# Output projection of an encoder block as seven products of halves, with block sums of weights made in DRAM and rows transposed once

## The chip, the cores and the metric

The kernel runs on one core of a Trainium2 chip. The metric is the device time of one execution in microseconds (us). TensorE (PE) multiplies matrices from SBUF into PSUM; VectorE (DVE), ScalarE (ACT) and GpSimd (POOL) do the elementwise work; SyncE (SP) issues most transfers. Each engine runs its own instructions in program order and waits on semaphores for the others.

## The reference

One layer of a hybrid encoder: 1024 tokens (a grid of 16 rows by 64 columns), width 1024, all in float32. Half of the mixed width is a gated depthwise convolution, half an attention over a window of 8 rows by 16 columns; both meet in one output projection. Cut to what matters:

```python
h = rms_norm(x, norm1_g)
z = h @ w_in                                   # conv a, gate; q, k, v
u = a * sigmoid(gate)
y = layer_norm(depthwise_conv31(u) + dw_bias, conv_ln_g, conv_ln_b)
conv = silu(y)                                 # (S, 512)
attn = neighbourhood_attention(q, k, v, rpb)   # (S, 512)
x = x + concat([conv, attn]) @ w_out           # output projection, (S, 1024) @ (1024, 1024)
h2 = rms_norm(x, norm2_g)
x = x + (silu(h2 @ w_gate) * (h2 @ w_up)) @ w_down   # inner width 2816
```

## The kernel before

Every float32 operand of the large products is split into a high and a low part (`split`, L103: a cast on ACT, a subtraction on POOL or DVE). `mac` (L110) makes a block product of three matmuls, 128x128 against 128x512: high by high, high by low, low by high.

**Order in time.** The program is one list written out by hand. norm1, the input projection and the convolution's taps fill the first 227 us; the taps run on DVE, some side taps on ACT and POOL (`side_taps`, L330). The loop at L789 is the attention: 32 steps (half a grid of rows, a block of columns, a pair of heads) in a pipeline. In iteration i, scores of step i are multiplied on PE (`score_mm`), those of step i-1 are scaled on POOL (`score_norm`, L637), those of i-2 are transposed on PE (`flip`, L646) and evacuated on DVE and ACT (`flip_out`, L651), step i gets its bias on DVE and its exponential on ACT (L628, L630), and step i-3 is multiplied with the values (`weigh`, L662). Every fourth step a result is evacuated (`evac_hi`, `evac_lo`). Weights of the output projection are loaded by SP (`issue`) and split in between (`take`, `take_parts`, L156).

**Output projection.** For each of 8 token tiles `t` and each half `d` of the width, `proj` (L723) runs over 8 blocks `k` of 128 (4 of the convolution, 4 of attention): 8 x 2 x 8 x 3 = 384 matmuls into one PSUM tile (`pj`, `pk`). Between its blocks `weave` inserts prepared work: `conv_T` transposes the convolution's output into rows (L728), `conv_stats` and `conv_scale` normalise it, `conv_silu` transposes it back. `resid` (L774) adds the result to the rows `x2`, once for each tile and half. `norm2` and `norm2_out` (L856, L863) make the normed rows `xn`. `t2_one` (L994) transposes the first four tiles (32 transposes).

**Gate and up.** The 1024x1024 by 1024 products of each pair of column blocks are made as seven products of halves, m1 to m7 (`product`, L1013; `evac`, L1024): on the rows' side they use A11, A12, A22 and the sums S1 to S4 (`s_sum`, made on rows, then transposed by `s_T`, L963, 80 transposes), on the weights' side sums of weight blocks made by DVE (`t_sums`, L893) and split (`prep`). The last stage does the same for the down projection.

## Time and profile before

| | us |
|---|---|
| median of three runs | 1064.31 (1063.71 to 1064.37) |
| the profiled execution | 1064.03 |
| its span | 1062.2 |
| PE busy | 1045.4 |
| DVE, ACT, POOL busy | 699.8, 443.7, 397.3 |

The stages follow each other on PE: up to about 227 us norm, projection and taps; to 317 attention; to 421 output projection and norm2; to 850 gate and up; to the end the down projection. Busy time is the time in which at least one instruction was under way; consecutive matmuls overlap, so the distance of their starts is what each of them takes. A row of the timeline gives start and duration in us, engine, line, operation, output<-inputs, shape, count of merged instructions, and in brackets the idle time before it and what ended it. A row of the groups gives count, then busy time in us and mean ns of one, then idle time before. A row of the windows gives for each engine busy us and instructions in the stretch, then the granted clock of PE as a share of full speed, the transfers' share and their rate.

### The profile page before, as it was taken

Reading aid. Unit: us, or ns where it says so; the run is one execution under the profiler, and the core shown is the slowest. Engines: PE = TensorE matmul, PEld = TensorE weight load, DVE = VectorE, ACT = ScalarE, POOL = GpSimd, SP = SyncE. Lnnn points to the kernel's source line nnn. Section 1 sums busy time; section 2 is a strip of 40 time slices with the busy share of each in tenths; the row PEclk is TensorE's granted clock in tenths of the full one; section 3 lists DMA queues with packets and bytes.
Section 4 is the critical chain, followed back from the end, with each engine's and each line's share of the span. In section 5 each row is a group of like instructions: output and inputs, shape, how many; then the busy total and the mean of one; then the engine's idle time right before and its main releaser. Section 6 shows DMA issues by size and latency. Waiting matters only on the chain.

```text
span 1062.2 us, 13969 instructions
## 1 busy us (share of the span) xinstructions
PE 1045.4 (98%) x5068; PEld 847.3 (80%) x5068; DVE 699.8 (66%) x1072; ACT 443.7 (42%) x874; POOL 397.3 (37%) x308
## 2 busy tenths in 40 slices
PE   7999999999999999999999999999999999999997
PEld 5788888776667888788888888888888888888886
DVE  6768998966765247666565564564655567858883
ACT  6456346626776334532323223332233344433441
POOL 0126568823542301444554544545454200002310
PEclk9999999999999999999999999999999999999999
DMA  9416681245504412032322222232132597634641
GB/s 333 164 47 225 217 257 36 75 161 154 165 34 161 136 80 99 21 129 77 136 91 104 109 99 95 104 129 100 70 131 78 194 322 276 209 99 132 205 127 43
DMA packets 68244, 144.05 MB, mean 136 GB/s; under 512 B 12496, under 2 KB 21200, under 8 KB 67536
## 3 DMA queue, kind: packets, MB, share of 16 engines
q1 hardware_dynamic: 66336, 139.95, 38.3%
q10 hardware_dynamic: 1840, 3.22, 0.9%
q8 instruction: 40, 0.66, 0.3%
q14 instruction: 28, 0.23, 0.1%
HBM read 103.99 MB, written 44.76 MB: 140 GB/s over the span
## 4 chain that ended last, share of the span: by engine, by line
PE 94%; DMA 2%; DVE 1%; ACT 1%; POOL 1%; issue 0%; SPq 0%; POOLq 0%; ACTq 0%
PE B L112 6%; PE B L114 6%; PE B L113 6%; PE A L112 4%; PE D L112 4%; PE D L114 4%; PE A L114 4%; PE D L113 4%; PE A L113 4%; PE z L113 3%; PE z L112 3%; PE z L114 3%; PE gl L114 3%; PE gl L112 3%; PE gl L113 3%; PE o L662 2%
## 5 line engine op out<-in xcount | busy, mean ns | idle before, releaser
L319 DVE SCALAR_TENSOR_TENSOR cv<-u,par,cv 128x1009 f32<-128x1009 f32 (+14 forms) x85 | 108.5, 1276 | 1.9
L345 POOL TENSOR_TENSOR pa<-pa,pr 128x1022 f32<-128x1022 f32 (+10 forms) x31 | 74.2, 2392 | 35.5 <-ACT pr L344 26.5
L104 ACT CAST op<-sr 128x512 fp32r<-128x512 f32 x77 | 47.7, 619 | 52.1 <-PE B2d L114 26.3
L108 DVE TENSOR_TENSOR op<-sr,op 128x512 fp32r<-128x512 f32 x77 | 57.1, 742 | 16.1 <-ACT op L104 16.0
L1037 DVE TENSOR_TENSOR g<-B,g 128x512 f32<-128x512 f32 x22 | 15.2, 691 | 79.0 <-PE B L114 79.0
L1209 POOL TENSOR_TENSOR ou<-ou,resm 128x512 f32<-128x512 f32 x8 | 12.2, 1530 | 144.0 <-DMA resm<-xd 142.1
L1046 ACT ACTIVATE D<-D 128x512 f32<-128x512 f32 x22 | 12.8, 582 | 113.1 <-DVE D L1045 113.1
L1032 DVE TENSOR_TENSOR u<-B,g 128x512 f32<-128x512 f32 x22 | 15.2, 691 | 62.1 <-PE B L114 62.1
L104 ACT CAST op<-wd 128x512 fp32r<-128x512 f32 x66 | 40.9, 620 | 30.7 <-DVE wd L1124 18.4
L637 POOL TENSOR_SCALAR e<-e,rs 128x288 f32<-128x288 f32 (+1 forms) x64 | 34.1, 545 | 50.2 <-DVE rs L635 42.9
L108 DVE TENSOR_TENSOR op<-wd,op 128x512 fp32r<-128x512 f32 x66 | 50.4, 764 | 1.8
L893 DVE TENSOR_TENSOR ts<-gu,ts 128x512 f32<-128x512 f32 x44 | 51.0, 1159 | 0.8
L1035 ACT ACTIVATE A<-A 128x512 f32<-128x512 f32 x20 | 11.6, 582 | 76.3 <-PE A L114 76.3
L630 ACT ACTIVATE e<-e,mx 128x288 f32<-128x288 f32 (+1 forms) x64 | 36.2, 569 | 2.0 <-DVE mx L628 2.0
L628 DVE CUSTOM_DVE_ANT_0 e<-s,tab 128x288 f32<-128x288 f32 (+1 forms) x64 | 30.1, 505 | 8.1 <-PE s L615 8.0
L344 ACT ACTIVATE pr<-u,par 128x1022 f32<-128x1022 f32 (+10 forms) x31 | 34.2, 1135 | 1.2 <-ACT vs L405 1.2
L893 DVE TENSOR_TENSOR ts<-gu 128x512 f32<-128x512 f32 x22 | 34.1, 1551 | 0.0
L646 PEld LDWEIGHTS p<-ident,e 128*96 128x96 f32 (+1 forms) x192 | 20.1, 133 | 15.2 <-issue 10.5
L944 POOL TENSOR_TENSOR xn<-xn,xn 128x512 f32<-128x512 f32 x4 | 6.9, 1732 | 57.3 <-DVE sn L944 57.3
L646 PE MATMUL p<-ident,e 128*96 128x128 f32 (+1 forms) x192 | 27.6, 280 | 0.7 <-DVE pT L651 0.6
L662 PE MATMUL o<-pT,vw 96*64 96x128 f32 (+1 forms) x384 | 28.0, 281 | 0.0
L615 PE MATMUL s<-kT,qT 64*128 64x288 f32 (+1 forms) x128 | 26.7, 495 | 0.0
(1039 smaller groups left out, 3449.6 us busy)
## 6 DMA issues: line engine op xcount, KB each, us to landing
gu<-in_gu SPq DMA_DIRECT2D x44, 512.0 KB
sr<-sd SPq DMA_DIRECT2D x77, 256.0 KB
sd<-sd SPq DMA_DIRECT2D x22, 512.0 KB
wd<-in_wd SPq DMA_DIRECT2D x44, 256.0 KB
sd<-g SPq DMA_DIRECT2D x33, 256.0 KB
x<-in_x SPq DMA_DIRECT2D x16, 512.0 KB
xd<-x SPq DMA_DIRECT2D x8, 512.0 KB
resm<-xd SPq DMA_DIRECT2D x16, 256.0 KB
```

The costliest lines, as they stand in the source:

```text
L104: act.copy(hi, src)
L108: eng.tensor_tensor(*[w[..., sl] for w in (lo, src, hi.bitcast(F32))], OP.subtract)
L112: pe.matmul(acc, lh, rh, start=start, stop=False, skip_group_check=True)
L113: pe.matmul(acc, lh, rl, start=False, stop=False, skip_group_check=True)
L114: pe.matmul(acc, ll, rh, start=False, stop=stop, skip_group_check=True)
L319: dve.scalar_tensor_tensor(acc[:, o], uc[:, i], dwk[:, c, t:t + 1], acc[:, o], OP.mult, OP.add)
L344: act.activation(pr[:, o], uc[:, i], AF.Copy, scale=dwk[:, c, t:t + 1])
L345: pool.tensor_tensor(pa[:, o], pa[:, o], pr[:, o], OP.add)
L630: act.activation(e[:, hh], e[:, hh], AF.Exp, bias=mx, scale=-1.0, accum_out=rs[:, hh:hh + 1])
L646: pe.transpose(pt[:m, g * P:(g + 1) * P], es[i][:, hh, g * m:(g + 1) * m], ident)
L662: pe.matmul(os_[s_][hh * HD:(hh + 1) * HD, hp], vw[cb, rh + g][:, c:c + HD], pTs[i][:, g, hh], start=g == 0, stop=g == 2)
L893: dve.tensor_tensor(o, l, r, OP.subtract)
```

## The change

**Seven products.** The output projection becomes seven products of halves, n1 to n7. On the activations' side: `a11` (attention of the second half of the grid rows), A22 and A12 (the convolution of the two halves) and four combinations Q1 to Q4, made of `rowf` (attention of the first half) and `diff` in place and split by POOL. On the weights' side the blocks B11, B21, B22 and sums P1 to P4. Each product is 4 tiles x 4 blocks x 3 matmuls, 336 in all; a result goes into one or two of the rows' halves (`put`, 40 instructions, where `resid` had 16).

**Block sums in DRAM.** P1 to P4 of the output weights (`w4`) and of the first four gate/up blocks (`g4`) are made in DRAM by `sum_steps`: SP copies one block (12 transfers: two halves for each sum of w4, one for each of g4), POOL adds another with an accumulating transfer (12 as well). P2 starts from P1 and P4 from P2, so these wait for each other; the steps stand iterations or products apart, by the numbers in the loops. `t_sums` then serves blocks 4 to 21 only, and all of `prep`'s splits go to POOL.

**Convolution norm.** Its transposes, statistics, inverse root (three Newton steps on DVE in place of ACT's root) and scaling stand in the attention loop. `conv_silu` stays in the projection, with 12 subtractions or additions that put it into `diff` and `rowf`.

**Rows transposed once.** `turn` transposes the normed rows of all tiles (64 transposes, 16 groups of 4); the sums S1 to S4 are made from the transposed copies by DVE and POOL, and `s_split` splits them. The first four gate/up blocks take their products in another order, and signs of some sums are turned.

```diff
...
+    def sum_steps(w, parts):
+        h = P // parts
+
+        def put_(n, m, i):
+            return lambda: nc.sync.dma_start(pw[w, n][i * h:i * h + h], block(w, m)[i * h:i * h + h])
+
+        def add(n, m, i):
+            return lambda: pool.dma_start(pw[w, n][i * h:i * h + h], block(w, m)[i * h:i * h + h], accum_op=OP.add,
+                                          max_dma_last_dim=2048)
+        both = range(parts)
+        head = [put_(n, "B12", i) for n in ("P1", "P3") for i in both]
+        head += [add(n, m, i) for n, m in (("P1", "B11"), ("P3", "B22")) for i in both]
+        tail = [f(n, m, i) for n, l, r in (("P2", "P1", "B22"), ("P4", "P2", "B21"))
+                for f, m in ((put_, l), (add, r)) for i in both]
+        head.insert(7, tail.pop(0)) if parts == 2 else None
+        return head + tail
...
-            at[cb] = [G(f"at{cb}{w}", F32R).rearrange("p (c t q) -> p c t q", c=4, t=2) for w in range(2)]
-        act.copy(at[cb][0][:, :, rh], os_[s_])
-
-    def evac_lo(s_, cs=slice(0, 4)):
+            if not rowf:
+                rowf.extend(G(f"rf{j}").rearrange("p (c b q) -> p c b q", c=2, b=4) for j in range(2))
+            for j in range(2):
+                act.copy(rowf[j][:, :, cb], os_[s_][:, 2 * j:2 * j + 2])
+        else:
+            a11[cb] = [w.rearrange("p (c q) -> p c q", c=4) for w in lr(G(f"a11{cb}", F32R))]
+            act.copy(a11[cb][0], os_[s_])
...
-        hi, lo = [w[:, cs, rh] for w in at[cb]]
-        dve.tensor_tensor(lo, os_[s_][:, cs], hi.bitcast(F32), OP.subtract)
+        if rh == 0:
+            return
+        if not diff:
+            diff.extend(G(f"df{j}").rearrange("p (c b q) -> p c b q", c=2, b=4) for j in range(2))
+        for j in js:
+            cs = slice(2 * j, 2 * j + 2)
+            hi, lo = [w[:, cs] for w in a11[cb]]
+            dve.tensor_tensor(lo, os_[s_][:, cs], hi.bitcast(F32), OP.subtract)
+            dve.tensor_tensor(diff[j][:, :, cb], os_[s_][:, cs], rowf[j][:, :, cb], OP.subtract)
...
+    LHS = {"n7": "Q3", "n4": "A22", "n6": "Q2", "n5": "Q1", "n2": "A12", "n3": "Q4"}
+    RHS = {"n1": "B11", "n7": "P3", "n4": "P4", "n6": "P2", "n5": "P1", "n2": "B21", "n3": "B22"}
+    CB = (0, 3, 1, 2)
+
+    def proj(p, cb, acc, cs=range(4), start=True):
+        w = wq[RHS[p]]
+        for c in cs:
+            mac(acc, lhs(p, c, cb), [w[:, o + c * 512:o + c * 512 + 512] for o in (0, 2048)],
...
+    def q_split(n, f, j, eng):
+        if j == 0:
+            qop[n] = H(n, F32R)
+        split(*[qop[n][:, o + j * 1024:o + j * 1024 + 1024] for o in (0, 2048)],
+              f[j].rearrange("p c b q -> p (c b q)"), (eng,))
...
+    mvs = par[:, 8:24].rearrange("p (t n) -> p t n", n=2)
...
+    def conv_norm(t):
+        y = conv_T(t)
+        st6 = SM(f"bs{t}", 6)
         dve.bn_stats(st6, y)
-        dve.bn_aggr(mv, st6)
-        act.activation(sd, mv[:, 1:2], AF.Sqrt, bias=eps)
-        cs[t] = y, mv, sd
-        if 1 <= t <= 4:
-            conv_scale(t - 1)
-        if t >= 4:
-            conv_scale(t)
-
-    def conv_scale(t):
-        y, mv, sd = cs.pop(t)
-        r = SM(f"br{t}", 1)
-        dve.reciprocal(r, sd)
+        dve.bn_aggr(mvs[:, t], st6)
         if t % 2 == 0:
-            xx = G(f"xh{t}")
-            xh.extend([xx[:, :512], xx[:, 512:]])
-        if t >= 6:
-            dve.tensor_scalar(xh[t], y, mv[:, 0:1], r, op0=OP.subtract, op1=OP.mult)
-        else:
-            nb = SM(f"bb{t}", 1)
-            dve.scalar_tensor_tensor(nb, mv[:, 0:1], -1.0, r, OP.mult, OP.mult)
-            act.activation(xh[t], y, AF.Identity, bias=nb, scale=r)
+            xh.extend(lr(G(f"xh{t}")))
+        act.copy(xh[t], y)
...
+    def rsqrt(out, v, name):
+        n = v.shape[-1]
+        w, g, q = SM(name + "w", n), SM(name + "g", n), SM(name + "q", n)
+        dve.tensor_scalar(w, v, EPS, None, op0=OP.add)
+        dve.tensor_scalar(g.bitcast(I32), w.bitcast(I32), 1, None, op0=OP.logical_shift_right)
+        dve.tensor_scalar(g.bitcast(I32), g.bitcast(I32), -1.0, float(0x5F3759DF), op0=OP.mult, op1=OP.add)
+        yield
+        for i in range(3):
+            if i == 2:
+                yield
+            dve.tensor_tensor(q, g, g, OP.mult)
+            dve.scalar_tensor_tensor(q, q, 0.25 ** i, w, OP.mult, OP.mult)
+            dve.scalar_tensor_tensor(g, q, -3.0, g, OP.add, OP.mult)
+        dve.tensor_scalar(out, g, -0.125, None, op0=OP.mult)
+        yield
+
+    def conv_scale(t, eng):
+        eng.tensor_scalar(xh[t], xh[t], mvs[:, t, 0:1], rc[:, t:t + 1], op0=OP.subtract, op1=OP.mult)
...
+    def conv_diff(h, c, y4):
+        tiles = lambda w: w.rearrange("p (b i j) -> p i b j", b=4, j=16)
+        d, r = [tiles(w[c // 2][:, c % 2].rearrange("p b q -> p (b q)")) for w in (diff, rowf)]
+        dve.tensor_tensor(d, y4, d, OP.subtract if h else OP.add)
+        if h == 0:
+            dve.tensor_tensor(r, r, y4, OP.subtract)
...
-    def resid(t, d, acc):
-        dve.tensor_tensor(x2[t][:, d * 512:(d + 1) * 512], acc, x2[t][:, d * 512:(d + 1) * 512], OP.add)
-
-    acc0, xh = [], []
-
-    def attn_half(t):
-        acc0.append(mm(f"pj{t}"))
-        proj(t, 0, acc0[t], range(4, 8))
-
-    def fill(*ks):
-        if not acc0:
-            act.activation(warm, eps, AF.Sqrt)
-            acc0.append(mm("pj0"))
-        proj(0, 0, acc0[0], ks)
+    def put(t, d, acc, op=OP.add, eng=dve):
+        w = x2[t][:, d * 512:(d + 1) * 512]
+        eng.tensor_tensor(w, w, acc, op)
...
+    def read(p, cb):
+        acc = pb[cb]
+        if p == "n1":
+            put(4 + cb, 0, acc)
+            put(4 + cb, 1, acc, OP.subtract)
+        elif p == "n7":
+            put(cb, 1, acc, OP.subtract)
+            put(cb, 0, acc)
+        elif p in ("n4", "n6"):
+            put(cb, 0, acc, OP.add if p == "n4" else OP.subtract)
+        elif p == "n5":
+            put(cb, 1, acc)
+            put(4 + cb, 1, acc)
+            norm2(cb)
+        elif p == "n2":
+            put(4 + cb, 0, acc)
+        else:
+            put(4 + cb, 1, acc)
+            norm2(4 + cb)
...
-        if i in (14, 22):
-            take_parts(jobs)
+        if i in (13, 17, 21, 25):
+            take_parts(jobs, more=i < 21)
+        if i in (2, 4, 9, 11, 16, 18):
+            aside_sum()
+        if i in (3, 6, 13, 21, 28):
+            gate_sum()
+        if i in (32, 33):
+            issue()
...
+        if i % 3 == 0 and i < 27:
+            conv_norm(i // 3 - 1)
+        if i == 25:
+            root = rsqrt(rc, mvs[:, :, 1], "rc")
+        if 25 <= i < 28:
+            next(root)
+        if 28 <= i < 32:
+            conv_scale(2 * i - 56, dve)
+            conv_scale(2 * i - 55, dve)
+        if i == 33:
+            act.activation(warm, eps, AF.Silu)
+            conv_silu(0, 0)
...
-    products = [(i, p) for p in ("m1", "m2", "m6", "m5", "m7", "m4", "m3") for i in range(2)]
-    products += [(i, p) for i in range(2, FB) for p in ORDER]
+    products = [(i, p) for k in (0, 2) for p in ("m1", "m2") for i in (k, k + 1)]
+    products += [(i, p) for k in (0, 2) for p in SRC for i in (k, k + 1)]
+    products += [(i, p) for i in range(4, FB) for p in ORDER]
...
+    def turn(t, j):
+        if not h2:
+            h2.extend(H(f"h2{w}", F32R).rearrange("p (k s) -> p k s", s=512) for w in range(2))
+        pt = (tp, mm)[j](f"t2{t}{j}")
+        for i in range(4):
+            kb = 4 * j + i
+            pe.transpose(pt[:, i * P:(i + 1) * P], xn[t][:, kb * P:(kb + 1) * P], ident)
+        if j == 0:
+            xT[t] = G(f"xT{t}")
+        w = lr(xT[t])[j]
+        if t < 4:
+            hi, lo = [q[:, 4 * j:4 * j + 4, t * P:(t + 1) * P] for q in h2]
+            p3 = pt.rearrange("p (k s) -> p k s", s=P)
+            act.copy(hi, p3)
+            act.copy(w, pt)
...
+    def group(p, cbs=CB):
+        for cb in cbs:
+            more = p in ("n7", "n5")
+            if not more:
+                pb[cb] = mm(f"{p}{cb}")
+            proj(p, cb, pb[cb], start=not more)
+            read(p, cb)
...
+    weaves(12, s0=lambda: (weigh(31), evac_hi(7), evac_lo(7)), s1=QS("Q3", diff, 0, pool), s2=lambda: tails.pop()(), s3=lambda: read("n1", 0),
+           s4=QS("Q3", diff, 1, pool), s6=C(0, 1), s10=take)
+    group("n1", CB[1:])
+    for cb in CB:
+        load_x2(cb)
+    gate_sum()
+    weaves(16, s1=C(0, 2), s5=take, s9=C(0, 3), s13=QS("Q2", diff, 0, pool))
+    group("n7")
+    weaves(16, s0=C(1, 0), s2=QS("Q2", diff, 1, pool), s4=take, s6=C(1, 1), s9=take, s12=QS("Q1", rowf, 0, pool))
+    group("n4")
+    gate_sum()
+    weaves(16, s0=C(1, 2), s2=take, s5=C(1, 3), s7=QS("Q1", rowf, 1, pool), s10=take, s13=QS("Q4", diff, 0, pool))
+    group("n6")
+    weaves(16, s1=take, s3=QS("Q4", diff, 1, pool), s6=take, s9=N(0), s13=N(3))
+    group("n5")
+    gate_sum()
+    while pos[0] < len(chunks):
+        issue()
+    for _ in range(3):
+        next_raw()
+    weaves(16, s0=take, s1=[N(1), U(0, 0)], s2=U(0, 1), s3=[lo2, lo2], s4=U(3, 0), s5=[U(3, 1), N(2)], s6=[lo2, lo2],
+           s7=U(1, 0), s8=U(1, 1), s9=[lo2, lo2, prep], s10=[U(2, 0), take], s11=U(2, 1), s12=[lo2, lo2], s13=prep)
+    group("n2")
+    weaves(16, s3=prep, s7=prep, s9=N(4), s12=U(4, 0), s13=[U(4, 1), N(7)], s15=SS(0, 1, 2))
+    group("n3")
...
+        0: dict(s0=U(7, 0), s1=[U(7, 1), N(5)], s2=SP("S2", 0), s3=SS(3, 1, 2)),
+        1: dict(s0=U(5, 0), s1=[U(5, 1), N(6)], s2=SP("S2", 3), s3=SS(1, 1, 2)),
+        2: dict(s0=U(6, 0), s1=[U(6, 1), lambda: act.activation(warm, eps, AF.Silu)], s2=SP("S2", 1), s3=SS(2, 1, 2)),
+        3: dict(s0=SP("S2", 2), s2=SP("S1", 0), s3=SP("S1", 3)),
...```

Three places in the engines' orders follow: instruction, output<-inputs, shape, count. First POOL in attention, iterations 15 to 18, before: score scalings (L637) with splits of the output weights between some.

```order
L637 TENSOR_SCALAR e14_2540<-e14_2540,rs14_2541 128x288 x2
L637 TENSOR_SCALAR e15_2574<-e15_2574,rs15_2575 128x288 x2
L108 TENSOR_TENSOR wo04_2523<-wo04r_1627,wo04_2523 128x256
L637 TENSOR_SCALAR e16_2607<-e16_2607,rs16_2608 128x384 x2
L108 TENSOR_TENSOR wo04_2523<-wo04r_1627,wo04_2523 128x256
L637 TENSOR_SCALAR e17_2641<-e17_2641,rs17_2642 128x384 x2
```

and after:

```order
L677 TENSOR_SCALAR e14_2609<-e14_2609,rs14_2610 128x288 x2
L118 TENSOR_TENSOR wB11_2558<-B110r_1637,wB11_2558 128x256
L212 DMA w4P4_68<-in_w4 256x512
L677 TENSOR_SCALAR e15_2644<-e15_2644,rs15_2645 128x288 x2
L118 TENSOR_TENSOR wB11_2558<-B110r_1637,wB11_2558 128x256
L677 TENSOR_SCALAR e16_2689<-e16_2689,rs16_2690 128x384 x2
L118 TENSOR_TENSOR wB11_2558<-B111r_1748,wB11_2558 128x256
L212 DMA w4P4_68<-in_w4 256x512
L677 TENSOR_SCALAR e17_2724<-e17_2724,rs17_2725 128x384 x2
```

A split stands in each iteration, and the two accumulating transfers of P4 (L212) stand ahead of the scaling of steps 15 and 17.

Second DVE in attention around step 28, before (bias with running maximum L628, flip evacuation L651, result evacuation L674) and after:

```order
L635 RECIPROCAL rs27_2975<-rs27_2975 128x2
L628 ISA e28_3007,mx280_3009<-s280_2991,tab11_2356 128x384
L628 ISA mx280_3009 128x1
L628 ISA e28_3007,mx281_3012<-s281_2993,tab11_2356 128x384
L628 ISA mx281_3012 128x1
L651 COPY pT26_3005<-p26_2998 128x3x128
L674 TENSOR_TENSOR at11_2824<-o5_2851,at10_2823 128x2x128
L635 RECIPROCAL rs28_3008<-rs28_3008 128x2
```

```order
L675 RECIPROCAL rs27_3112<-rs27_3112 128x2
L668 ISA e28_3152,mx280_3154<-s280_3136,tab11_2396 128x384
L668 ISA mx280_3154 128x1
L668 ISA e28_3152,mx281_3157<-s281_3138,tab11_2396 128x384
L668 ISA mx281_3157 128x1
L691 COPY pT26_3150<-p26_3143 128x3x128
L836 TENSOR_SCALAR xh0_2208<-xh0_2208,par_93 128x512 x2
L727 TENSOR_TENSOR a111_3091<-o5_2964,a111_3091 128x256
L728 TENSOR_TENSOR df1_2507<-o5_2964,rf1_2330 128x2x128
L675 RECIPROCAL rs28_3153<-rs28_3153 128x2
```

Two scalings of the convolution (L836) and one subtraction more (L728) stand ahead of the next reciprocal.

Third PE at the head of the first product m6, before: the operand S2 is transposed (L963) between the product's blocks.

```order
L112 MATMUL B0_4107<-S2_4054,t0m6_4075 128x512
L113 MATMUL B0_4107<-S2_4054,t0m6_4075 128x512
L114 MATMUL B0_4107<-S2_4054,t0m6_4075 128x512
L963 MATMUL sq_4112<-ident_84,sn0_3878 128x128
L963 MATMUL sq_4112<-ident_84,sn1_3936 128x128
L963 MATMUL sq_4112<-ident_84,sn2_3985 128x128
L963 MATMUL sq_4112<-ident_84,sn3_4019 128x128
L112 MATMUL B0_4107<-S2_4054,t0m6_4075 128x512
```

After, m6 has matmuls alone, and the transposes stand in the product n2 of the output projection:

```order
L1068 MATMUL t230_3846<-ident_92,xn3_3779 128x128 x4
L122 MATMUL n23_3842<-wB21_3702,A12_3529 128x512
L123 MATMUL n23_3842<-wB21_3702,A12_3529 128x512
L124 MATMUL n23_3842<-wB21_3702,A12_3529 128x512
L1068 MATMUL t231_3857<-ident_92,xn3_3779 128x128 x4
```

The normed rows themselves (xn) are transposed there, two groups for each tile.

360 lines of the change are left out of this document (183 added, 177 removed).

## The prediction

> **What bounds the kernel now.** I read the page first: busy shares and the chain that ended last.
>
> ```profile
> PE 1045.4 (98%) x5068; PEld 847.3 (80%) x5068; DVE 699.8 (66%) x1072; ACT 443.7 (42%) x874; POOL 397.3 (37%) x308
> PE 94%; DMA 2%; DVE 1%; ACT 1%; POOL 1%; issue 0%; SPq 0%; POOLq 0%; ACTq 0%
> ```
>
> TensorE (PE) is busy 98% of the span and makes up 94% of the chain. A share over the whole span hides stages with other limits, so the second view is the table of windows: attention (first two), the output projection, its end with norm2, and the gate/up products.
>
> ```profile
> core 0: us, PE busy (x) PEld busy (x) DVE busy (x) ACT busy (x) POOL busy (x), PEclk, DMA share, GB/s
> 270.00:280.00 10.00, 10.00 (x92) 6.46 (x92) 7.73 (x27) 7.83 (x26) 5.29 (x10) 1.00 0.57 166
> 300.00:310.00 10.00, 10.00 (x91) 6.37 (x90) 7.55 (x26) 8.01 (x26) 6.05 (x11) 1.00 0.02 6
> 360.00:370.00 10.00, 10.00 (x46) 8.29 (x45) 1.38 (x2) 0.00 (x0) 2.40 (x2) 1.00 0.76 241
> 390.00:400.00 10.00, 9.44 (x51) 7.64 (x50) 5.40 (x8) 4.23 (x8) 0.00 (x0) 1.00 0.14 55
> 500.00:520.00 20.00, 20.00 (x90) 16.57 (x89) 12.35 (x17) 5.50 (x10) 9.68 (x8) 1.00 0.33 122
> ```
>
> PE is full in every stage that the change touches, at a granted clock of 1.00. Two things differ. In attention VectorE (DVE) is at 77% and ScalarE (ACT) at 80%: PE is the bound there with little room. In the projection DVE is at 14%: there is much room. So an instruction taken from PE is worth its time, and one added elsewhere costs only what exceeds the room of its stage. What is one PE instruction worth? Its listed duration (0.39 us) overlaps its neighbours'; what counts is the distance from start to start:
>
> ```profile
> 331.12 0.40 PE L112 MATMUL pj<-wo,at 128*128 128x512 f32 x1
> 331.35 0.39 PE L113 MATMUL pj<-wo,at 128*128 128x512 f32 x1
> 331.58 0.39 PE L114 MATMUL pj<-wo,at 128*128 128x512 f32 x1
> 331.81 0.60 PE L728 MATMUL y<-ident,u 128*128 128x128 f32 x4
> 332.17 0.48 PE L112 MATMUL pj<-wo,at 128*128 128x512 f32 x1
> 332.48 0.39 PE L113 MATMUL pj<-wo,at 128*128 128x512 f32 x1
> ```
>
> 331.12 to 331.81 is three matmuls: 0.23 us each. A group of four transposes takes 331.81 to 332.17, 0.36 us, and the matmul behind it 0.31 instead of 0.23: 0.44 us for a group.
>
> **What is removed.** (1) The output projection had 8 token tiles x 2 halves x 8 blocks x 3 = 384 matmuls of 128x512. Now it has 7 products x 4 tiles x 4 blocks x 3 = 336. 48 fewer x 0.23 = **11.0 us**. (2) Transposes of the normed rows and their block sums: 32 + 80 before, 64 now, so 48 fewer, in 12 groups: 12 x 0.44 = **5.3 us**. The convolution's transposes only move from the projection into attention; PE is full in both, so they cost the same there. (3) PE stalls of the old order, such as
>
> ```profile
> 431.02 0.40 PE L112 MATMUL B<-S,t0m 128*128 128x512 f32 x1
> 431.73 0.50 PE L113 MATMUL B<-S,t0m 128*128 128x512 f32 x1 [0.31 <-DVE S L108]
> ```
>
> where the next start is 0.71 us away instead of 0.23: half a microsecond lost to an operand that was transposed and split just ahead of its product. The window 390 to 400 loses 0.56 the same way. In the new order transposes stand a product or more ahead of their use. Three or four such gaps: **2 us** (0 to 3). Together 18.3 us.
>
> **What is added in attention.** One iteration, by engine in time:
>
> ```profile
> 290.43 0.17 DVE L635 RECIPROCAL rs<-rs 128x2 f32<-128x2 f32 x1 [0.65 <-ACT e L630]
> 290.55 0.56 DVE L628 CUSTOM_DVE_ANT_0 e<-s,tab 128x384 f32<-128x384 f32 x1
> 291.03 0.55 DVE L628 CUSTOM_DVE_ANT_0 e<-s,tab 128x384 f32<-128x384 f32 x1
> 291.74 0.56 DVE L651 COPY pT<-p 128x384 f32<-128x384 f32 x1
> 292.22 0.41 DVE L674 TENSOR_TENSOR at<-o,at 128x256 fp32r<-128x256 f32 x1
> 292.94 0.17 DVE L635 RECIPROCAL rs<-rs 128x2 f32<-128x2 f32 x1 [0.31 <-ACT e L630]
> ...
> 290.76 1.15 POOL L637 TENSOR_SCALAR e<-e,rs 128x384 f32<-128x384 f32 x2 [0.60 <-DVE rs L635]
> 293.27 1.14 POOL L637 TENSOR_SCALAR e<-e,rs 128x384 f32<-128x384 f32 x2 [1.37 <-DVE rs L635]
> 295.75 0.73 POOL L108 TENSOR_TENSOR wo<-wo06r,wo 128x256 fp32r<-128x256 f32 x1 [1.33 <-ACT wo L104]
> ...
> 292.72 0.88 PE L646 MATMUL p<-ident,e 128*128 128x128 f32 x6
> 295.18 0.88 PE L646 MATMUL p<-ident,e 128*128 128x128 f32 x6
> ```
>
> The period is 2.46 us (292.72 to 295.18). DVE needs 290.43 to 292.63 of it, 2.2 us, with its evacuation (L674); without that and the short wait at 291.6, 1.65 us. So it has 0.3 to 0.8 us to spare. The chain to watch: reciprocal on DVE, scaling on GpSimd (POOL), flips on PE. POOL's scaling ends at 291.91, the flips start at 292.72: 0.8 us of slack. What comes in, from the nearest rows:
>
> ```profile
> L735 DVE BATCH_NORM_STATS2 bs<-y 128x6 f32<-128x512 f32 x8 | 5.6, 695 | 2.4 <-PE y L728 2.4
> 332.17 0.81 DVE L752 TENSOR_SCALAR xh<-y,bm,br 128x512 f32<-128x512 f32 x1
> ```
>
> - Statistics, 8 times in every third iteration: 0.70 us and a small aggregate of about 0.18; PE grows by 0.44 in the same iteration. 1.65 + 0.88 is below 2.46 + 0.44: hidden. Where they meet an evacuation on DVE too, about 0.1 is lost.
> - The second row half's evacuation gets one subtraction more of 256 columns (0.41 us, as L674), the first half's loses its own: 2.2 + 0.4 still is near 2.46 + a little.
> - The inverse root is 13 small DVE instructions, which the reciprocal prices at 0.17: up to six in one iteration, about 1.0 us on top of 1.65 and an evacuation. It exceeds by 0 to 0.6 us in each of two iterations.
> - Scaling is two 128x512 instructions in each of four iterations. The row above has 0.81 us with a PSUM source; a plain SBUF source is shown by no such row, so 0.41 (half the width, L674) to 1.49 (the dearest 512-wide DVE row, below) bound it. I take 0.7: 1.65 + 1.4 + 0.8 (where subtraction and difference fall) against 2.46 exceeds by 0.6 to 1.4.
>
> These together: **2.2 us** (0 to 8, the upper end with scalings of 1.49 us: 4 x 1.6 more).
>
> Six accumulating transfers are issued by POOL in attention, ahead of a scaling instruction in its order. POOL issues no transfer before, so nothing there gives its price. Nearest rows: what SP needs to issue one, and POOL's own longest ordinary instruction.
>
> ```profile
> 308.74 0.37 SPq L141 DMA_DIRECT2D wo14r<-in_wo  x1
> 332.81 0.89 SPq L141 DMA_DIRECT2D wo10r<-in_wo  x1
> L108 POOL TENSOR_TENSOR w23l<-w23r,w23h 128x1024 fp32r<-128x1024 f32 x1 | 2.4, 2399 | 0.0
> ```
>
> With 1.15 us of scaling in a period of 2.46, POOL has 1.3 us free, and the flips have 0.8 us of slack. At 0.37 the six cost nothing; at 1.0 us each about 0.2: 1.2 in all; at 2.4 each (2.4 - 0.8) x 6 = 9.6. I take 1.0, near the row of 0.89, as both are issues of transfers: **1 us** (0 to 10). [...]
>
> In the value stage four more stand on POOL ahead of the last side taps:
>
> ```profile
> 208.97 7.29 POOL L345 TENSOR_TENSOR pa<-pa,pr 128x1014 f32<-128x1014 f32 x3 [0.52 <-ACT pr L344]
> 228.15 1.22 DVE L324 TENSOR_TENSOR u<-cv,pa 128x1024 f32<-128x1024 f32 x1
> ```
>
> The taps end at 216.3 and DVE uses them at 228.15: 12 us of cover against 4 x 2.4 at worst. Nothing. Two more follow in the projection; they are counted with its POOL work.
>
> **What is added in the projection and behind it.** The result reads into the residual rows are 40 instead of 16, 24 x 0.69 = 16.6 us more on DVE:
>
> ```profile
> L775 DVE TENSOR_TENSOR x<-pk,x 128x512 f32<-128x512 f32 x8 | 5.5, 687 | 6.0 <-PE pk L114 6.0
> ```
>
> The seven products last 7 x 48 x 0.23 = 77 us, and that stage had DVE at 14%; by group I count at most 11 us of DVE work beside 11 to 14 us of PE work (the longest: n1 with the last attention tile's evacuation, n2 with four groups of transposes). POOL has four operand splits and weight splits of 1024 columns in most groups, 4 x 2.4 = 9.6 us (or, with a transfer of 1 us, 10.6) beside 11.0. Everything is hidden, but the reserve is thin, and there is a row that says such a reserve can vanish:
>
> ```profile
> 388.19 0.69 DVE L893 TENSOR_TENSOR ts<-gu 128x512 f32<-128x512 f32 x1
> 499.99 1.77 DVE L893 TENSOR_TENSOR ts<-gu,ts 128x512 f32<-128x512 f32 x1
> ...
> 499.48 1.74 POOL L108 TENSOR_TENSOR t4m<-gu,t4m 128x512 fp32r<-128x512 f32 x1
> ```
>
> The same DVE operation takes 0.69 us where POOL is idle (388.19) and 1.77 where POOL subtracts beside it (499.99). So a DVE instruction with SBUF sources next to POOL's splits costs up to 1.1 us more, on both engines' account. The new order puts some of these together: block sums on transposed rows, norm2's scaling. Some 20 of them x 1.1 = 22 us of engine time spread over 120 us, nearly all under PE; I take **1 us** (0 to 5). ACT has 53 casts and copies more and 15 activations less; at 80% in attention I take **0.5 us** (0 to 2). The first gate/up tiles lose 16 DVE sums and only read other memory: nothing.
>
> [...]
>
> **Sum.** The profiled execution's own time is 1064.03 us, 0.3 below the median of 1064.31, so the two can stand for each other. 1064.0 - 11.0 - 5.3 - 2 + 2.2 + 1 + 1 + 0.5 = 1050.4; I predict **1050 us**, 1.3% less.
>
> **Rivals.**
> *A, nothing new stalls.* All additions lie under PE: 1064.0 - 18.3 = about 1046. For it: DVE at 14% in the projection, 0.8 us of flip slack. Against: DVE's 2.2 of 2.46 us in attention. 0.12.
>
> *B, attention becomes bound by DVE and POOL.* If the eight scalings take 1.49 us, if they and the splits that POOL now makes in every iteration stretch each other as at 499.99, POOL's scaling of the scores comes late to the flips. The waits of the old order show how near that is (columns: us in all, number, longest):
>
> ```profile
> PEld p L646 <- POOL e L637: 4.4, 8, 0.5
> ```
>
> Eight waits of PE for POOL, 4.4 us in all, so the flips sometimes wait already. With 16 splits between iterations 13 and 28 and half a microsecond for each, 8 us come on top of the forecast: 1056 to 1062. For it: that row. Against: a 256-wide split of 0.73 us fits POOL's 1.3 free. 0.18.
>
> *C, the accumulating transfers hold POOL.* This one ends slower. POOL runs in order; behind each of the six stand the score scalings of the iteration, and behind these the flips, weighing and all of PE. If POOL is held c us by each, PE loses about 6 x (c - 0.8), plus what the two in the projection push out. The change saves 18.3 and gives back 3.7 elsewhere, so 14.6 are left: it is slower from 6 x (c - 0.8) = 14.6, c = 3.2 us. At c = 4 it is 1064.0 - 14.6 + 19 = 1069. For it: nothing shows what an accumulating transfer of 512 KB to 1 MB asks of POOL. Against: SP issues one of 512 KB in under 0.9. 0.10.
>
> *D, the change doesn't shorten the end.* The removed PE time returns as waits for weights: SP's queue also runs in order, and a copy that waits for an accumulation holds the loads behind it. Attention has at least five iterations, 12 us, between a step and the one that needs it; if an accumulation needs 15 us more than that, the 14.6 are gone: 1064. Against: the windows show the transfers' share at 0.02 to 0.76, so there is room. 0.06.
>
> **How the numbers follow.** Forecast (1047 to 1055) 0.54, A 0.12, B 0.18, C 0.10, D 0.06. The range reaches from A with its best stall term, 1064.0 - 11.0 - 5.3 - 3 = 1044.7, say 1044, to the end of B, 1062; C and D, 0.16, lie outside. Differences under 0.2% (2.1 us) can't be told from no change by such a measurement. Faster by more: forecast, A and B, 0.84. Within it: D, 0.06. Slower: C, 0.10.
>
> **What the changed profile would show.** PE has 48 matmuls of 128x512 and 48 of 128x128 fewer, still 0.23 us apart. An iteration stays near 2.46 us (2.9 where a transpose group is in it); if those with a transfer on POOL are longer, by how much is c. The scalings' duration tells 0.7 from 1.49. PE windows from 310 to 460 show 10.00 of 10 with a few tenths missing; more than 1 us missing in a window of the projection says that DVE or POOL arrive late (B), and a wait for a load there says D. I am wrong in the main point if PE's starts in the projection are further apart than 0.23 us, or if the gate/up stage, which I take as unchanged but for its head, has become longer.

## The result and the profile after

The changed kernel takes 1076.47 us (median of 4, 1074.28 to 1077.93) against 1064.01 us for the kernel before on the same chip: ratio 1.0116, interval 1.0098 to 1.0134. It is 1.2% slower where 1.3% faster was forecast. First the page of the profiled execution (span 1074.2 us): busy shares, and the chain that ended last.

```profile
PE 1031.5 (96%) x4972; PEld 834.8 (78%) x4972; DVE 720.4 (67%) x1097; ACT 463.9 (43%) x911; POOL 453.4 (42%) x342
PE 85%; DVE 4%; issue 4%; ACT 2%; POOL 2%; DMA 1%; SPq 0%; POOLq 0%; DVEq 0%; ACTq 0%
```

PE has 96 instructions fewer (5068 to 4972), 48 matmuls and 48 transposes, and is busy 14 us less; that part of the forecast came true. But PE holds only 85% of the chain instead of 94%: the time saved, and more, is spent waiting. Where? The table of windows over attention (columns as before: PE, PEld, DVE, ACT, POOL, granted clock, transfers' share, GB/s):

```profile
260.00:270.00 10.00, 10.00 (x101) 7.05 (x102) 8.03 (x32) 7.74 (x24) 5.21 (x10) 1.00 0.52 176
270.00:280.00 10.00, 6.42 (x60) 4.01 (x56) 4.58 (x16) 6.47 (x21) 3.43 (x7) 1.00 0.87 220
280.00:290.00 10.00, 0.00 (x0) 0.00 (x0) 0.00 (x0) 0.00 (x0) 0.00 (x0) 0.54 0.85 284
290.00:300.00 10.00, 2.93 (x19) 2.19 (x20) 1.27 (x5) 1.14 (x4) 3.71 (x6) 0.50 0.46 134
300.00:310.00 10.00, 9.42 (x76) 5.63 (x74) 6.98 (x25) 7.37 (x22) 6.47 (x10) 0.94 0.96 272
```

From about 277 to 295 us every engine stands still and only transfers run. When PE comes back, the granted clock is 0.50 (290 to 300). The timeline of POOL (start, duration, in brackets the idle time before and its end) and of PE shows who waits:

```profile
274.71 0.73 POOL L118 TENSOR_TENSOR wB<-B110r,wB 128x256 fp32r<-128x256 f32 x1 [0.88 <-ACT wB L114]
295.56 0.90 POOL L212 DMA_DIRECT2D w4P<-in_w  x1 [20.13 <-DMA w4P<-w4P]
...
275.51 0.92 PE L655 MATMUL s<-kT,qT 64*128 64x384 f32 x4
297.07 1.52 PE L686 MATMUL p<-ident,e 128*96 128x128 f32 x6 [20.65 <-POOL e L677]
```

POOL stood 20.1 us at the accumulating transfer of P4 in iteration 16: it needs the copy of P2 into P4, which had not landed. The scaling of the scores is behind it, the flips behind that. The issue itself takes 0.90 us. And the copy was late because of SP's queue:

```profile
252.40 19.60 SPq L640 DMA_DIRECT2D vw<-vd  x4
272.04 5.46 SPq L209 DMA_DIRECT2D g4P<-in_g  x1
...
278.22 1.17 SPq L209 DMA_DIRECT2D w4P<-w4P  x2
279.47 16.23 SPq L640 DMA_DIRECT2D vw<-vd  x4
295.81 4.61 SPq L151 DMA_DIRECT2D P30r<-w4P  x1
```

The two copies of P4 (w4P<-w4P) stand in the program at iterations 9 and 11; they were issued at 278 us, when iteration 16 already waited, and landed 17 us later. Ahead of them SP stood 19.6 us at the loads of a values' window (vw), then at a copy of 1 MB.

### The profile page after: what moved, and what is told of

The parts are those of the page before. It is cut to its first block, busy times and chain, and to the rows that moved or that the text cites. A ratio compares the mean times of both kernels' runs of the same rounds, so it can differ in the third digit from the quotient of the medians.

```text
span 1074.2 us, 13901 instructions
## 1 busy us (share of the span) xinstructions
PE 1031.5 (96%) x4972; PEld 834.8 (78%) x4972; DVE 720.4 (67%) x1097; ACT 463.9 (43%) x911; POOL 453.4 (42%) x342
## 4 chain that ended last, share of the span: by engine, by line
PE 85%; DVE 4%; issue 4%; ACT 2%; POOL 2%; DMA 1%; SPq 0%; POOLq 0%; DVEq 0%; ACTq 0%
PE B L122 5%; PE B L123 5%; PE B L124 5%; PE D L122 4%; PE D L123 4%; PE D L124 4%; PE A L122 3%; PE A L123 3%; PE A L124 3%; PE z L123 3%; PE z L122 3%; PE z L124 3%; PE gl L124 3%; PE gl L122 3%; PE gl L123 3%
## 5 line engine op out<-in xcount | busy, mean ns | idle before, releaser
L114 ACT CAST op<-sr 128x512 fp32r<-128x512 f32 x77 | 47.6, 619 | 52.9 <-PE B2d L124 22.3
L118 DVE TENSOR_TENSOR op<-sr,op 128x512 fp32r<-128x512 f32 x77 | 59.3, 770 | 15.6 <-ACT op L114 15.6
L114 ACT CAST op<-wd 128x512 fp32r<-128x512 f32 x66 | 40.9, 619 | 30.8 <-DVE wd L1284 18.4
L668 DVE CUSTOM_DVE_ANT_0 e<-s,tab 128x288 f32<-128x288 f32 (+1 forms) x64 | 29.7, 500 | 35.0 <-POOL e L677 21.7
L677 POOL TENSOR_SCALAR e<-e,rs 128x288 f32<-128x288 f32 (+1 forms) x64 | 35.7, 595 | 39.6 <-DVE rs L675 36.8
L686 PE MATMUL p<-ident,e 128*96 128x128 f32 (+1 forms) x192 | 29.1, 285 | 24.0 <-POOL e L677 21.2
L686 PEld LDWEIGHTS p<-ident,e 128*96 128x96 f32 (+1 forms) x192 | 20.4, 135 | 40.5 <-POOL e L677 33.8
L118 DVE TENSOR_TENSOR op<-wd,op 128x512 fp32r<-128x512 f32 x66 | 50.6, 766 | 1.8
L990 DVE TENSOR_TENSOR ts<-ts,gu 128x512 f32<-128x512 f32 x36 | 43.3, 1203 | 0.6
L874 DVE TENSOR_TENSOR x<-x,n 128x512 f32<-128x512 f32 x40 | 26.0, 681 | 15.7 <-PE n L124 12.4
L691 ACT COPY pT<-p 96x384 f32<-96x384 f32 (+1 forms) x32 | 15.3, 478 | 37.9 <-PE p L686 36.5
L990 DVE TENSOR_TENSOR ts<-gu 128x512 f32<-128x512 f32 x18 | 30.0, 1666 | 0.0
L702 PE MATMUL o<-pT,vw 96*64 96x128 f32 (+1 forms) x384 | 28.7, 286 | 0.0
```

The lines of the kernel that those rows point to most:

```text
L114: act.copy(hi, src)
L118: eng.tensor_tensor(*[w[..., sl] for w in (lo, src, hi.bitcast(F32))], OP.subtract)
L677: pool.tensor_scalar(es[i][:, hh], es[i][:, hh], rs[:, hh:hh + 1], 1.0, op0=OP.mult, op1=OP.mult)
L686: pe.transpose(pt[:m, g * P:(g + 1) * P], es[i][:, hh, g * m:(g + 1) * m], ident)
L990: dve.tensor_tensor(lr(tsum[i, 1])[n - 3] if o is None else o, l, r, OP.add)
```

## The experiments

Twelve kernels were run, all built from the changed one. Those without all their sums (e3, e7, e10) read plain blocks instead, so they time the work and do not compute the layer. Times are medians; the ratio is to the kernel before on the same chip.

| run | us | ratio, 95% interval |
|---|---|---|
| e1, P4's adds later | 1079.81 | 1.0150, 1.0135 to 1.0165 |
| e2, P4's copies ahead of the held loads | 1085.24 | 1.0202, 1.0187 to 1.0217 |
| e3, no sums | 1058.39 | 0.9952, 0.9935 to 0.9969 |
| e4, gate sums later | 1074.37 | 1.0100, 1.0085 to 1.0115 |
| e5, window loads later | 1071.32 | 1.0072, 1.0057 to 1.0087 |
| e6, and P3's load early | 1075.22 | 1.0109, 1.0094 to 1.0124 |
| e7, as e6 without sums | 1054.53 | 0.9918, 0.9901 to 0.9934 |
| e8, all sums early | 1068.08 | 1.0052, 1.0033 to 1.0070 |
| e9, and norm spread | 1066.41 | 1.0036, 1.0018 to 1.0055 |
| e10, as e6 without gate sums | 1057.16 | 0.9948, 0.9931 to 0.9966 |
| e11, P1 and P3 of the gate early, norm spread | 1058.23 | 0.9951, 0.9937 to 0.9965 |
| e12, and S4 on DVE | 1057.06 | 0.9946, 0.9930 to 0.9963 |

### First theory: the order of one queue

The reading above says: one late copy, one waiting add. Two kernels move one or the other, one leaves the sums out, one takes 2 MB of copies from in front. e1:

```diff
-        if i in (2, 4, 9, 11, 16, 18):
+        if i in (2, 4, 9, 11, 24, 27):
```

> Only the place of two POOL instructions changes: the accumulating transfers of P4 stand in iterations 24 and 27 instead of 16 and 18. Theory (queue order): the changed kernel lost 20.6 us because POOL stood at the first of them, waiting for a copy that SP had issued late, plus about 2 us in which PE came back at a lower clock. Then this kernel takes 1076.5 - 22.6 = 1054 us (1050 to 1057), faster than before. Rival (volume): the 16 MB of additional transfers slow everything wherever they stand; then it stays above 1068. Rival (engines): the work added on DVE and ACT in attention is what costs; then it stays above 1068 as well, and a stall of PE is seen without POOL's wait.

Not as the theory said: 1079.8, 3 us above the changed kernel. POOL no longer waits for the add, but PE stands still twice for other things (7.8 and 12.8 us). ACT's timeline of e1 shows the second:

```profile
314.52 0.40 ACT L114 CAST wP<-P30r 128x256 fp32r<-128x256 f32 x1 [14.53 <-DMA P30r<-w4P]
```

The load of P3 (P30r), issued at 296 us, had not landed at 300; ACT waits 14.5 us in its order, with the evacuations of the flips behind it. In the changed kernel this load was late too, but its wait lay under POOL's. e2:

```diff
+        if i == 6:
+            aside_sum()
+            aside_sum()
         if i in (6, 12):
             load_window(i // 6)
```

> The adds stay in iterations 16 and 18; the two copies of P4 are put on SP's queue ahead of the loads of iteration 6, one of which waits for its buffer, instead of behind them in iterations 9 and 11. Theory (queue order): the copies land before iteration 16 and POOL waits no more: 1054 us (1050 to 1058). If the accumulation of P2 or the copy itself were too slow for the distance (rival: transfers too slow), POOL still waits over 8 us and the time is over 1063.

1085.2, 31 us above the expected 1054 and the slowest of all. The copies left at 253 us and POOL's wait for them is gone, but now a bias table behind the window loads is late. One row of the waits of e2 (us in all, number, longest):

```profile
DVE e L668 <- DMA tab<-tf: 16.7, 2, 16.4
```

PE also waits 8.5 us for the window loads themselves and 12.1 us behind the load of P3.

e3, which reads plain blocks in place of the sums:

```diff
-        return a[w][BLK[n]] if n in BLK else pw[w, n]
+        return a[w][BLK[n] if n in BLK else int(n[1]) - 1]
...
-        return head + tail
+        return [lambda: None for _ in head + tail]
```

> All 24 transfers of the block sums are left out; P1 to P4 are read from the plain blocks, so the sums are not computed. Theory (queue order): this is e1 less six issues on POOL and their share of the memory: 1052 us (1048 to 1055), within 4 us of e1. Rival (volume): clearly below e1, by 10 us or more. Rival (engines): still above 1065.

1058.4: the block sums cost 18.1 us (1076.5 less 1058.4), and all the rest of the change gains only 5.6 (1064.0 less 1058.4). Against the forecast for this kernel (1052) some 6 us are missing. Over half of that is one stall, by the timeline of PE:

```profile
291.08 0.88 PE L686 MATMUL p<-ident,e 128*128 128x128 f32 x6
297.12 1.54 PE L686 MATMUL p<-ident,e 128*128 128x128 f32 x6 [3.51 <-POOL e L677]
301.65 1.54 PE L686 MATMUL p<-ident,e 128*128 128x128 f32 x6
```

Even without sums the load of P3 comes late, since SP holds it behind the window loads, until 276.7 us. The wait is 3.5 us, and the same six transposes take 1.54 us instead of 0.88 in the two iterations behind it. e4:

```diff
-        if i in (3, 6, 13, 21, 28):
+        if i in (17, 19, 22, 25, 30):
```

> The gate/up blocks' sums move back, from iterations 3, 6, 13, 21 and 28 to 17, 19, 22, 25 and 30, so that 2 MB of copies no longer stand ahead of P4's copies; those still stand behind the held load. Theory (queue order, with the queue's bytes as second part): SP comes free at 272 us as before, P4's copies then need 6 to 10 us less, and POOL's wait shrinks from 20 to between 6 and 13 us: 1060 to 1070. If the held load alone made the wait, it shrinks only by the 5.5 us that SP spent issuing a copy there: 1071. If the bytes alone made it: 1054 to 1057.

1074.4, above every expected value and 2 us below the changed kernel. PE's wait itself shrank from 20.7 to 11.0 us, as the theory said, and new ones came behind it, by e4's timeline of PE:

```profile
289.66 1.51 PE L686 MATMUL p<-ident,e 128*96 128x128 f32 x6 [11.02 <-POOL e L677]
312.13 1.46 PE L686 MATMUL p<-ident,e 128*128 128x128 f32 x6 [3.24 <-POOL e L677]
```

So the first theory names the wait that ended last, but not what makes it: whichever transfer is put first, another is late by as much.

### Second theory: loads that hold the queue

SP stood 19.6 and 16.2 us at window loads, and the theory was that their buffers were not free. e5 issues them later, when the buffers are about free; e6 also issues P3's load early; e7 is e6 without sums.

```diff
-        if i in (6, 12):
-            load_window(i // 6)
+        if i in (14, 17):
+            load_window(1 if i == 14 else 2)
...
-        if i in (32, 33):
+        if i in (8, 32, 33):
             issue()
```

> The loads of the values' windows (four each) move on SP's queue from iterations 6 and 12 to 14 and 17, where their buffers are about free; all sums stay. Theory (held queue): SP stood 19 us and 16 us at these loads, and everything behind them came late: the bias table, P4's copies, the load of P3, one after the other the next stall. Here table and copies are issued before 262 us, so POOL's wait for P4 (20 us) and the waits for the table go. P3's first load is still issued only an iteration before its cast, so a stall of 5 to 10 us with its lower clock stays: 1060 us (1055 to 1068). Rival (volume): the transfers are too many for this stage in any order: above 1070.

> As e5, and the first load of P3 is issued in iteration 8. Theory (held queue): no transfer is waited for in attention any more; the time is that of e3 (1058.4) less its own 3.5 us wait for this load and about as much at the lower clock behind it, plus some 2 us for POOL's issues: 1054 us (1050 to 1058), faster than before. Rival (volume): above 1062.

> As e6 without any transfer of the sums (P1 to P4 are read from the plain blocks, so the sums are not computed). Theory (held queue): 1051 us (1048 to 1054), 1 to 5 us below e6, which is then what the sums cost in a good order. Rival (volume): e6 lies 10 us or more above it.

Without sums the theory nearly holds: e7 has 1054.5, just above its range and 3.9 us below e3, and attention runs without a late load. With sums it fell: 1071.3 and 1075.2, and e6 lies 20.7 us above e7, as the rival (volume) had it. Nor was it mainly the buffers that held SP. Of the 19.6 us in the changed kernel, 13.4 are the issue of a single load (first row below). The same four loads, issued late, held SP for 22.3 us in e6 (second row) and 6.8 in e7 (third row), and these two differ by the sums alone:

```profile
258.63 13.36 SPq L640 DMA_DIRECT2D vw<-vd  x1
...
265.08 22.33 SPq L640 DMA_DIRECT2D vw<-vd  x4
...
262.56 6.82 SPq L640 DMA_DIRECT2D vw<-vd  x4
```

The sums lengthen such an issue but do not make it: the longest in the kernel before took 10.2 us. In e6 SP was free to issue P4's copies at 259 us, 19 us earlier than in the changed kernel, and POOL still waited, by e6's SP and POOL timelines and its windows:

```profile
259.16 3.86 SPq L209 DMA_DIRECT2D w4P<-w4P  x2
...
283.36 0.91 POOL L212 DMA_DIRECT2D w4P<-in_w  x1 [6.96 <-DMA w4P<-w4P]
```

```profile
250.00:260.00 10.00, 10.00 (x98) 7.08 (x96) 7.40 (x27) 7.36 (x25) 3.96 (x8) 1.00 0.89 278
260.00:270.00 10.00, 10.00 (x97) 6.93 (x96) 8.02 (x32) 7.84 (x24) 5.04 (x9) 1.00 1.03 408
270.00:280.00 10.00, 7.38 (x70) 4.79 (x67) 5.44 (x21) 6.86 (x22) 4.12 (x7) 0.95 0.93 267
```

The copies needed up to 20 us to land, while the transfer engines are full from 250 to 280 us (shares of 0.89, 1.03 and 0.93). By the sizes in the page, the row issued there is a copy of 1 MB, a bias table of 1.5, a copy of 1, a load of 0.5, a table of 1.5 and P4's copies of 1: 6.5 MB, the copies being both read and written. The rates of the three windows add up to 9.5 MB.

### Third theory: the transfers fill this stage

If volume is the cause, it helps to take transfers out of attention, not to reorder them. e10 leaves the gate/up blocks' sums out of e6; e8 puts all 24 earlier; e9 adds a spread norm to e8. e10:

```diff
-        return head + tail
+        return [lambda: None for _ in head + tail] if w == "g4" else head + tail
```

> As e6, but the transfers of the gate/up blocks' sums are left out (their P1 to P4 are read from the plain blocks, so these sums are not computed); the sums of the output weights stay where they are. Theory (volume): 2 MB of copies and as much of adds less ahead of P4's copies: most of e6's 20.7 us go, 1058 (1055 to 1063). Rival (the chain of dependent transfers is too slow whatever stands beside it): above 1068.

1057.2, as expected: of e6's 20.7 us, 18.1 are gone with half of the sums' bytes, while the output weights' chain of dependent transfers is unchanged. The engines are full from 250 to 270 us only (0.99 and then 0.88), and P4's adds waited for nothing:

```profile
260.00:270.00 10.00, 9.40 (x92) 6.51 (x91) 7.16 (x28) 7.35 (x23) 3.49 (x8) 1.00 0.88 340
270.00:280.00 10.00, 9.54 (x91) 6.20 (x89) 6.54 (x26) 7.82 (x24) 7.75 (x13) 1.00 0.42 126
```

e8, in the projections of keys, queries and values (the names count the steps of `sum_steps`):

```diff
+        if t == 4:
+            bsum("w0", "w1", "w2", "w3", "g0", "g1")
...
+        if t == 5:
+            bsum("w4", "w5", "w6")
+        if t == 7:
+            bsum("w8", "g2", "g3")
...
+        bsum(*{1: ("w7", "w9"), 3: ("g4",), 4: ("w10",), 5: ("w11",), 6: ("g5",)}.get(t, ()))
...
+        bsum(*{0: ("w12", "w13"), 1: ("g6",), 4: ("w14",), 5: ("w15",), 7: ("g7",)}.get(t, ()))
```

> All 24 transfers of the sums stay, but stand early: the independent copies behind the last gate weight, where SP and the transfer engines are idle from 40 to 60 us, their adds from 66 us on, P2 in the projection stage, P4 in the value stage; none in attention. Window loads and P3's load as in e6. Theory (volume): in attention the transfer engines were full from 250 to 280 us (6.5 MB of tables, copies and loads in a row), so whatever was last in the row was waited for; with this order attention has only e7's transfers: 1054.5 us as e7 plus 0 to 4, so 1056 (1053 to 1060), faster than before. Rival (accumulating transfers cost wherever they stand, by POOL or by the memory): above 1066.

1068.1, in the rival's range. Attention has no late transfer any more, but six adds now run while SP makes the bias tables, by over a hundred small transfers, many of which wait for earlier ones; these come later, and the projection's weights behind them on SP too (the load w01r is issued at 140.0 us, in the changed kernel at 123.3). A wait and a window of e8:

```profile
ACT w01h L114 <- DMA w01r<-in_qkv: 13.9, 1, 13.9
...
150.00:160.00 10.00, 3.72 (x7) 2.12 (x7) 9.20 (x9) 6.26 (x7) 6.54 (x4) 0.66 0.94 294
```

The volume was moved to another stage with a queue of dependent transfers, and was paid there. e9:

```diff
+    CN, CS = (5, 6, 7, 8, 9, 10, 13, 14), (18, 21, 22, 23, 24, 25, 26, 29)
...
-        if i % 3 == 0 and i < 27:
-            conv_norm(i // 3 - 1)
+        if i in CN:
+            conv_norm(CN.index(i))
-        if i == 25:
+        if i == 15:
             root = rsqrt(rc, mvs[:, :, 1], "rc")
-        if 25 <= i < 28:
+        if 15 <= i < 18:
             next(root)
-        if 28 <= i < 32:
-            conv_scale(2 * i - 56, dve)
-            conv_scale(2 * i - 55, dve)
+        if i in CS:
+            conv_scale(CS.index(i), dve)
```

> As e8, and the convolution's norm is spread over attention: the statistics in iterations without a result subtraction, the inverse root in 15 to 17 and one scaling in each of eight iterations. Theory (DVE is the bound of the last iterations): the 1.9 us that PE lost between 300 and 320 us in e7 go, and some tenths elsewhere: 2 us below e8. Rival (the norm was hidden anyway): as e8.

1.7 us below e8. The runs of e9 scatter (1063 to 1073) and the intervals of the two overlap, so the time alone doesn't settle it. The traces do: from 260 to 340 us PE loses 2.9 us in e8 and 1.1 in e9.

e11 puts together what held: P1 and P3 of the gate/up blocks copied and added in the idle stretch from 40 to 60 us, ahead of the bias tables, the rest of the gate sums as in the change, the order of e6, the norm of e9. Nothing is left out. In the projection of keys and in attention:

```diff
+        if t == 4:
+            gate_sum(2)
         project(1, t, head_post)
+        if t == 4:
+            gate_sum(2)
...
-        if i in (3, 6, 13, 21, 28):
+        if i == 28:
             gate_sum()
```

> Nothing is left out. As e6 with two moves: P1 and P3 of the gate/up blocks are copied behind the last gate weight and added ahead of the fifth tile's split, where SP, POOL and the transfer engines are idle from 40 to 60 us (their P2 and P4 stay in iteration 28 and behind n1, n4, n5); and the norm is spread as in e9. Theory (volume in attention): e10's 1057.2, 2 us less for the norm, up to 3 us more for the transfers kept: 1057 us (1054 to 1060), faster than before. Rival (accumulating transfers cost wherever they stand): these two delay the bias tables as the ten of e8 did, and the time is 1062 or more.

1058.2, as expected, 0.5% faster than the kernel before and 1.7% faster than the change as given. Its windows show what is left:

```profile
280.00:290.00 10.00, 8.10 (x72) 4.81 (x70) 8.04 (x32) 6.86 (x20) 7.64 (x12) 1.00 0.76 182
310.00:320.00 10.00, 10.00 (x88) 6.77 (x86) 7.17 (x23) 7.13 (x23) 5.97 (x11) 1.00 0.47 143
420.00:430.00 10.00, 8.81 (x44) 7.08 (x43) 8.34 (x9) 5.91 (x11) 3.41 (x3) 1.00 0.01 2
440.00:450.00 10.00, 8.09 (x35) 6.10 (x34) 8.67 (x8) 7.39 (x14) 10.00 (x9) 1.00 0.19 52
```

At the head of gate and up (420 to 460) PE loses some 4 us, with POOL busy all the time in part of it. There POOL makes S4:

```profile
436.46 4.63 POOL L1039 TENSOR_TENSOR s<-xT,sn 128x256 f32<-128x256 f32 x4
442.75 4.16 POOL L1039 TENSOR_TENSOR s<-xT,sn 128x256 f32<-128x256 f32 x4
```

e12 gives this to DVE:

```diff
-        5: dict(..., s2=SS(0, 4, eng=pool), s3=SS(3, 4, eng=pool)),
-        6: dict(s0=SS(1, 4, eng=pool), s1=SS(2, 4, eng=pool), ...),
+        5: dict(..., s2=SS(0, 4), s3=SS(3, 4)),
+        6: dict(s0=SS(1, 4), s1=SS(2, 4), ...),
```

> As e11, but the 8 subtractions that make S4 run on DVE instead of POOL, where they took 8.8 us in the stretch in which POOL was busy all the time and PE lost some 4 us at the head of the gate/up stage. Theory (POOL bounds that head): 2 us below e11's 1058.2, so 1056 (1054.5 to 1057.5). Rival (DVE and POOL hold each other there, and DVE is as full): 1058 to 1060.

1057.1, inside the theory's range (1054.5 to 1057.5), but 1.2 us below e11 and not 2, and the intervals overlap, so a gain is not shown. The window at 440 loses 0.2 us less than in e11, and the one behind it is full (10.00 of 10):

```profile
440.00:450.00 10.00, 8.29 (x37) 6.26 (x36) 10.00 (x15) 8.47 (x17) 8.92 (x5) 1.00 0.37 105
```

DVE is now the full one there, so the work of that stretch seems too much for both.

## Why the prediction was wrong, step by step

**What PE is relieved of** was right: 48 matmuls and 48 transposes, and gate and up at the old pace (20.00 of 20 us busy in its windows before and after). The 16.3 us were there to be had.

**Old stalls, 2 us**, were sized too large. The windows of the kernel before at the place of the quoted stall:

```profile
420.00:430.00 10.00, 9.88 (x52) 7.80 (x51) 6.44 (x10) 6.30 (x11) 3.30 (x2) 1.00 0.14 54
430.00:440.00 10.00, 9.58 (x50) 7.18 (x49) 8.71 (x12) 5.18 (x10) 1.29 (x1) 1.00 0.00 1
```

0.12 and 0.42, with the 0.56 that the prediction had, are 1.1 us. And the 0.56 are not a stall of the same kind: PE waited there for a normed row of `norm2` (xn), which the new order doesn't cure; in e7 this wait is 1.19 us.

**DVE in attention, 2.2 us**, was right in kind and size. In e7, which has no sums to disturb it, PE loses 1.9 us where root and scalings stand (first two rows; the others belong to the next term):

```profile
300.00:310.00 10.00, 9.55 (x82) 5.49 (x81) 9.52 (x36) 7.34 (x22) 6.85 (x11) 1.00 0.17 54
310.00:320.00 10.00, 8.60 (x74) 6.17 (x74) 9.53 (x32) 7.17 (x22) 5.07 (x10) 1.00 0.43 134
410.00:420.00 10.00, 8.81 (x47) 7.07 (x47) 7.80 (x9) 7.77 (x16) 2.81 (x2) 1.00 0.13 51
420.00:430.00 10.00, 9.61 (x43) 7.64 (x42) 7.51 (x9) 7.26 (x15) 3.78 (x3) 1.00 0.19 63
430.00:440.00 10.00, 9.54 (x43) 7.55 (x41) 9.34 (x9) 5.35 (x10) 10.00 (x9) 1.00 0.28 89
440.00:450.00 10.00, 8.15 (x34) 6.18 (x35) 8.96 (x10) 7.06 (x13) 10.00 (x8) 1.00 0.32 103
```

DVE is at 95% there. The two prices came out on either side. By the changed kernel's timeline of DVE, two scalings take 0.98 us together, 0.49 each and not 0.7, while five of the root's 13 small instructions take 0.5 to 0.73 and not 0.17 (the last section shows when):

```profile
330.37 0.73 DVE L832 TENSOR_SCALAR par<-rcg 128x8 f32<-128x8 f32 x1
...
333.16 0.98 DVE L836 TENSOR_SCALAR xh<-xh,par 128x512 f32<-128x512 f32 x2
```

With the work spread, the window 310 to 320 of e11 is full, but the root still costs something where it stands now:

```profile
281.75 0.85 PE L691 MATMUL p<-ident,e 128*128 128x128 f32 x6 [0.78 <-DVE rcq L834]
```

**DVE beside POOL behind the projection, 1 us**, was a mis-sized term. The last four windows of e7 above lose 3.9 us. The prediction counted engine time over 120 us and took nearly all of it as hidden; but PE's five waits fall into 30 us (416 to 445) at the end of the projection and the head of gate and up: 1.2 us for the normed row, 1.2 for two results evacuated by ACT and DVE, 1.5 for two splits. How much of this comes from DVE and POOL lengthening each other, the runs don't show apart.

**POOL's issues, 1 us at c = 1.0**: the price was right (a median of 0.89 us for 512 KB and 1.04 for 1 MB), and as a price of the issue c stayed below the 3.2 of rival C's formula. C as written did not happen.

**Dependent transfers, 0 us**, is the step that failed. The sum has no term for them. The prediction dismissed them in rival D with two sentences: "Attention has at least five iterations, 12 us, between a step and the one that needs it" and "the windows show the transfers' share at 0.02 to 0.76, so there is room". The first takes a place in the program for a time on the queue: the copies stood seven iterations ahead of their add and were issued after it was due. The second reads room out of shares that the change then filled: in the changed kernel the windows from 260 to 310 have 0.52, 0.87, 0.85, 0.46 and 0.96. What happened has D's cause (the queue of SP) and C's effect (POOL held, once, for 20 us), at a chance of 0.16 for both together. Its sign for late loads (D) looked at the windows from 310 to 460 us; the changed kernel loses 20.7 us of PE's time from 270 to 300.

Put together for e7, by its terms: 1063.4 (the kernel before beside it) - 11.0 - 5.3 - 1.1 + 1.9 + 3.9 + 0.5 = 1052.3; measured 1054.5, the profiled execution 1052.3, the lowest of its four. The 0.5 is the prediction's term for ACT, which no run shows apart. PE loses 1.0 us more in e7 from 270 to 300, mostly waiting for POOL's scaling; with it the sum is 1053.3, and 1.2 us of the median stay unexplained. The other 20 us or so of the changed kernel are the transfers: 18.1 by e3, 20.7 by e6 against e7.

e6 is 4 us slower than e5, though only one load moved. This load now stands ahead of P4's copies, whose issue begins 2.4 us later (259.16 and not 256.81), and PE's wait behind P4's add grew from 4.2 to 7.5 us.

What stays open: whether copies or adds weigh more was not tried apart; nor was the place of the gate sums' copies in SP's queue told apart from their bytes, since e10 and e11 take both from in front of P4's copies and no run puts them behind these in e6's order.

## What to carry to other kernels

When a change adds transfers between dependent steps, draw up the queue that issues them and the bytes in flight in that stretch, with a time for each; a distance in iterations says nothing if an older load holds the queue or the engines are full (here seven iterations ended in a wait of 20.1 us). When the wait that ended last is moved and the time stays, look for the transfers behind it in the same row: leaving them all out (e3, e7) tells in one run what the row costs. The cure is to put the independent part into a stretch in which queue and engines are both idle, and to see who else uses that queue there.
